# Moving a quarter of a depthwise convolution and its norms beside the attention over a paged cache

## The chip, the cores and the metric

The kernel runs on one core of one Trainium2 chip. The metric is the device time of one execution in microseconds (us), as the median of several runs. In the profile the engines are PE (TensorE, with PEld for its weight loads), DVE (VectorE), ACT (ScalarE), POOL (GpSimd) and SP (SyncE, which issues DMAs). Each engine works through its own list of instructions in order, and engines wait for one another at semaphores.

## The reference

One decoder layer serves a prompt of 1024 rows and 8 sample rows with the same weights. The part that the change touches is the mixer: attention heads (MLA) beside a convolution group, joined by the projection `w_o`.

```python
qn, qr, c_kv, k_r, u = mixer_inputs(xp, ...)          # u: gated 512 channels
attn = mla_prompt(qn, qr, c_kv, k_r, w_uk, w_uv)      # 8 heads over 1024 rows, causal
conv = silu(layer_norm(depthwise_causal_conv(u_ext, conv_w) + conv_b, g, b))   # 31 taps, 512 channels
mix = concatenate([attn, conv]) @ w_o
mk, mv = mem_kv(mem_prompt, w_xk, w_xv)               # 256 memory rows, wanted later by a cross attention
# the 8 sample rows: the same mixer, but the attention reads a paged cache of 4096 past rows a sample,
#   s = q_lat . past_c + q_rope . past_r ;  p = softmax(s) ;  o_lat = p . past_c ;  o = o_lat . w_uv
# then: layer norm, cross attention, layer norm, feed-forward 1024 -> 4096 -> 1024, layer norm
```

All inputs and results are float32. A product of the prompt is made from two rounded parts of each factor (high and low) in three matmuls (`mm3`, lines 150 to 152).

## The kernel before

The program has stages that follow each other; times are from the profiled execution.

1. Projections, 0 to 212 us. PE forms `u`, the latent `cn`, and the queries `qn` (tile `pq`). DVE works through the convolution beside it: `mix<-u,convw,mix`, line 417, one instruction a tap over 128 channels and 1024 rows, 31 taps for each of `NCT` = 4 quarters of the channels (the first tap of a quarter is a `tensor_scalar`, 30 are `scalar_tensor_tensor`), and rotates the queries (lines 356 to 359).
2. Prompt attention, 243 to 439 us (the block `c3`): 8 heads by 8 row tiles, with two-part copies of the latent (`LH`, `LL` from the transposes `trl`), of keys and of probabilities. Five of the nine norms of the convolution (`conv_norm`) are put in at the steps `CLN`. A norm is four transposes of `mix` into a PSUM bank (`tl`, line 427), a copy by ACT (`cln`), row statistics and scaling by DVE with two small POOL instructions (`clr`), four transposes back (`tl`, line 435) and a copy by ACT.
3. Attention over the paged cache, 439 to 723 us (the block `c2`). 16 steps n, two for each sample b (halves e = 0, 1 of its 4096 cache rows). A step transposes cache rows (`trc`, 32 transposes of 128x128, copied by ACT and DVE in turn to `ct`; `trr` for the rotary part), makes half of a product of the memory keys or values (`mk`, 24 matmuls; its weights `kraw` come by DMA, POOL makes `kwh`, DVE `kwl`), and the scores (`main`). After every second step comes the softmax of a sample, a generator in pieces that the loop puts between other work: ACT copies `main` to `mr`, PE gathers it (`st`), DVE takes the maximum (`mx`, `m`, `md`, `ma`) in turns with PE, then `E_`, its sum `sm`, and `sa`. `values(b)` is the product of `E_` with the cache rows (`pv`, 64 matmuls) and a short gathering product (`pv<-summ,ob`). Step 0 also holds `absorb` (query products `tqs`, `tcs`, `tuk`, `tql`, `tsn`) and `memory_in` (transposes `trm`). Two of the other four norms stand in steps 11 to 14, two in a 17th pass of the loop behind the last scores, where the last softmax and values(7) stand too.
4. `silu` over the normed convolution: the first 640 columns just behind the prompt attention, the others behind the load of `w_o`.
5. The projection `w_o` (tile `po`) from 723 us on. It needs `XHb` and `XLb`, the two parts of `mix` (`split_mix`), and the two parts `w_oh`, `w_ol` of its weights. Memory cross attention and feed-forward follow, unchanged.

In the paged loop PE's order is written out by hand (`manual_schedule`); the order of the other engines comes from a scheduler that goes by priorities in program order, and `issue_after(x)` holds an instruction behind x. A PSUM bank belongs to a tag in each stage: `Banks(tr=3, main=1, st=1, pv=1, mk=1, tl=1)` in the loop, so a second tile of a tag with one bank waits until the first one has been copied out. A generator's `next` is one piece of its work; `run(soft)` advances a pending softmax by one piece, `run(ends)` finishes a `values`.

Of the kernel before, what the change touches and what calls it, by code (L numbers as in the profile page):

```python
# [53 lines left out]
CLN = (2, 8, 14, 20, 26)  # L54
# [51 lines left out]
def decoder_step(ctx: ExitStack, tc: tile.TileContext, I: dict, O: dict):  # L106
# [96 lines left out]
    with ExitStack() as c1:  # L203
# [137 lines left out]
        nc.sync.dma_start(O["new_conv_s"][0, :, 0:CK - 2, :], I["state_conv"][0, :, 1:CK - 1, :])  # L341

# [70 lines left out]
        for ct, u in enumerate(us_):  # L413
            acc = mixC[:, ct, 0:S]
            V.tensor_scalar(acc, u[:, 0:S], convw[:, ct, 0:1], cvec[:, 0, ct:ct + 1], op0=ALU.mult, op1=ALU.add)
            for j in range(1, CK):
                V.scalar_tensor_tensor(acc, u[:, j:j + S], convw[:, ct, j:j + 1], acc, op0=ALU.mult, op1=ALU.add)  # L417
            v = mixC[:, ct, S:NT]
            V.scalar_tensor_tensor(v, us[:, ct, :], convw[:, ct, CONV_S:CK], v, op0=ALU.mult, op1=ALU.add)
            V.tensor_scalar(v, v, cvec[:, 0, ct:ct + 1], None, op0=ALU.add)  # L420
# [37 lines left out]
    with ExitStack() as c3:  # L458
# [145 lines left out]
        for n in range(len(seq) + LAG):  # L604
# [28 lines left out]
        with tc.issue_after(mla_end[-1].ins):  # L633
            silu(0, len(CLN) * P)


    with ExitStack() as c2:
# [33 lines left out]
        def absorb():  # L671

            t = ps.tile([P, H, DB], F32, tag="tr", name="tqs")
# [3 lines left out]
            t = ps.tile([P, 3, DB], F32, tag="tr", name="tcs")  # L677
# [5 lines left out]
            for k in range(2):  # L683
                for g in range(2):
                    t = ps.tile([P, 4, P], F32, tag="tr", name="tuk")
# [37 lines left out]
        def columns(b, e):  # L723

            ct = de.tile([P, 2, 4, 512], F32, tag="ct", name="ct")
            for c in range(4):
# [32 lines left out]
        def softmax(b):  # L759
# [27 lines left out]
            sm = dp.tile([P, H], F32, tag="sm", bufs=2, name="sm")  # L787
# [78 lines left out]
        norms = [conv_norm(i, dp, ps, "tl", 2) for i in range(len(CLN), NTL + 1)]  # L866
# [5 lines left out]

        with tc.manual_schedule(engines={mybir.EngineType.PE}):
            for n in range(2 * DB + 1):
                b, e = divmod(n, 2)
                cols = columns(b, e) if b < DB else iter(())
                run(soft)
                next(cols, None)
                if b == DB:
                    norm()  # L880
                run(soft)
                next(cols, None)
                if b == DB:
                    norm()
# [797 lines left out]
```

## Time and profile before

| | |
|---|---|
| median of 3 runs | 1824.02 us (1823.56 to 1827.28) |
| profiled execution | 1826.9 us, of which 1825.1 us span |
| PE busy | 1686.1 us (92%), 12820 instructions |
| DVE busy | 1256.7 us (69%) |
| ACT busy | 614.7 us (34%) |
| POOL busy | 404.4 us (22%) |
| mean granted TensorE clock | 0.961 |

PE is busy 92% of the span. A busy share is a mean over all stages; in a table of the stages (busy time of each engine in a stretch of the span, and the granted clock) one sees in which of them PE waits, and the waits of PE in such a stretch name the engine that came last. A row of the timeline gives the start, the duration, the engine, the line, the operation, the tile written and those read, the count of alike instructions, and in brackets the idle time before and what ended it.

### The profile page before, as it was taken

Reading aid. Unit: us, or ns where it says so; the run is one execution under the profiler, and the core shown is the slowest. Engines: PE = TensorE matmul, PEld = TensorE weight load, DVE = VectorE, ACT = ScalarE, POOL = GpSimd, SP = SyncE. Lnnn points to the kernel's source line nnn. Section 1 sums busy time; section 2 is a strip of 40 time slices with the busy share of each in tenths; the row PEclk is TensorE's granted clock in tenths of the full one; section 3 lists DMA queues with packets and bytes.
Section 4 is the critical chain, followed back from the end, with each engine's and each line's share of the span. In section 5 each row is a group of like instructions: output and inputs, shape, how many; then the busy total and the mean of one; then the engine's idle time right before and its main releaser. Section 6 shows DMA issues by size and latency. Waiting matters only on the chain.

```text
span 1825.1 us, 32021 instructions
## 1 busy us (share of the span) xinstructions
PE 1686.1 (92%) x12820; PEld 1530.9 (84%) x12820; DVE 1256.7 (69%) x2166; ACT 614.7 (34%) x1283; POOL 404.4 (22%) x456
## 2 busy tenths in 40 slices
PE   8999669997899986999999999999999899999995
PEld 8999657886677764888988788999999899998995
DVE  4899988885444445766558576987777666667666
ACT  4112147775222222211134212333333344434322
POOL 0045033223021312311026311222332210002012
PEclk9999879998799997999999999999999999999998
DMA  6211000006155632323324721345444677877744
GB/s 199 58 48 41 1 24 1 1 5 239 58 205 200 253 135 98 128 105 129 121 82 139 248 105 48 117 135 160 148 137 151 202 263 263 289 264 254 249 143 151
DMA packets 154432, 255.38 MB, mean 140 GB/s; under 512 B 12998, under 2 KB 88174, under 8 KB 150179
## 3 DMA queue, kind: packets, MB, share of 16 engines
q1 hardware_dynamic: 146939, 210.56, 34.5%
q0 software_dynamic: 7344, 42.78, 6.2%
q8 instruction: 101, 1.65, 0.4%
q14 instruction: 48, 0.39, 0.1%
HBM read 207.66 MB, written 46.11 MB: 139 GB/s over the span
## 4 chain that ended last, share of the span: by engine, by line
PE 78%; DVE 10%; DMA 6%; ACT 3%; issue 2%; POOL 1%; SPq 0%; DVEq 0%; POOLq 0%; ACTq 0%
PE pd L151 4%; PE pd L152 4%; PE pd L150 4%; PE po L150 3%; PE po L151 3%; PE po L152 3%; PE ua L150 3%; PE ua L152 3%; PE ua L151 3%; PE trc L733 2%; PE px L151 2%; PE px L150 2%; DMA kraw<-in_w_xk 2%; PE px L152 2%; DMA ar<-in_w_down 2%
## 5 line engine op out<-in xcount | busy, mean ns | idle before, releaser
L151 PE MATMUL pd<-bl,ah 128*128 128x252 f32 (+1 forms) x768 | 219.7, 286 | 11.5 <-DVE bl L143 11.3
L150 PE MATMUL pd<-bh,ah 128*128 128x252 f32 (+1 forms) x768 | 219.3, 286 | 5.2 <-ACT bh L137 4.3
L152 PE MATMUL pd<-bh,al 128*128 128x252 f32 (+1 forms) x768 | 218.4, 284 | 1.8 <-DVE al L143 1.8
L151 PEld LDWEIGHTS pd<-bl,ah 128*128 128x128 f32 x768 | 147.3, 192 | 14.0 <-DVE bl L143 13.7
L150 PEld LDWEIGHTS pd<-bh,ah 128*128 128x128 f32 x768 | 147.2, 192 | 5.6 <-ACT bh L137 4.6
L152 PEld LDWEIGHTS pd<-bh,al 128*128 128x128 f32 x768 | 147.3, 192 | 2.0 <-DVE al L143 2.0
L417 DVE SCALAR_TENSOR_TENSOR mix<-u,convw,mix 128x1024 f32<-128x1024 f32 x120 | 148.9, 1273 | 0.1
L143 DVE TENSOR_TENSOR al<-ar,ah 128x1024 fp32r<-128x1024 f32 x48 | 63.7, 1328 | 72.1 <-ACT ah L137 69.9
L137 ACT CAST ah<-ar 128x1024 fp32r<-128x1024 f32 x48 | 50.3, 1048 | 160.8 <-PE pd L151 125.9
L1309 POOL TENSOR_TENSOR us<-uraw 128x512 f32<-128x512 f32 x28 | 43.7, 1579 | 233.2 <-DMA uraw<-in_w_up 163.7
L143 DVE TENSOR_TENSOR uhl<-uraw,uhl 128x512 fp32r<-128x512 f32 x50 | 50.4, 1011 | 45.6 <-ACT uhl L137 45.5
L143 DVE TENSOR_TENSOR bl<-br,bh 128x1032 fp32r<-128x1032 f32 (+2 forms) x64 | 74.1, 1159 | 6.8 <-ACT bh L137 6.8
L733 PE MATMUL trc<-ident,craw 128*128 128x128 f32 x512 | 67.7, 288 | 10.1 <-ACT ct L137 7.0
L733 PEld LDWEIGHTS trc<-ident,craw 128*128 128x128 f32 x512 | 58.2, 147 | 19.2 <-ACT ct L137 7.2
L565 POOL TENSOR_SCALAR pr<-pr,sm 128x384 f32<-128x384 f32 (+4 forms) x64 | 47.9, 750 | 112.5 <-DVE sm L564 67.0
L137 ACT CAST bh<-br 128x1032 fp32r<-128x1032 f32 (+2 forms) x64 | 60.6, 946 | 36.2 <-PE pd L152 27.5
L137 ACT CAST XHb<-tr 128x512 fp32r<-128x512 f32 x32 | 17.7, 588 | 155.4 <-PE tr L957 155.4
L1460 DVE TENSOR_TENSOR hs<-h,h 128x516 f32<-128x516 f32 x80 | 65.6, 851 | 4.6 <-DMA hc<-hs 4.5
L152 PE MATMUL ub<-XHb,uhl 128*128 128x252 f32 (+1 forms) x240 | 67.6, 282 | 0.0
L150 PE MATMUL ub<-XHb,uhl 128*128 128x252 f32 (+1 forms) x240 | 67.6, 282 | 0.0
L151 PE MATMUL ub<-XLb,uhl 128*128 128x252 f32 (+1 forms) x240 | 67.5, 281 | 0.0
L143 DVE TENSOR_TENSOR kwl<-kraw,kwh 128x512 fp32r<-128x512 f32 x32 | 22.1, 691 | 65.3 <-POOL kwh L140 65.3
(550 smaller groups left out, 5744.3 us busy)
## 6 DMA issues: line engine op xcount, KB each, us to landing
ar<-in_w_down SPq DMA_DIRECT2D x96, 512.0 KB, 5.4
br<-hc SPq DMA_DIRECT2D x48, 516.0 KB, 4.6
hc<-hs SPq DMA_DIRECT2D x75, 258.0 KB, 2.1
uraw<-in_w_up SPq DMA_DIRECT2D x32, 512.0 KB, 6.0
X<-x SPq DMA_DIRECT2D x16, 512.0 KB, 2.6
kt<-in_cache_mem_k SPq DMA_DIRECT2D x32, 256.0 KB, 2.9
vsr<-in_cache_mem_v SPq DMA_DIRECT2D x32, 256.0 KB, 2.8
hc<-h SPq DMA_DIRECT2D x30, 258.0 KB, 2.4
```

What stands on the lines that cost most here:

```text
L137: return A.copy(dst, src)
L143: return (V if eng == "v" else G).tensor_tensor(dst, src, ff(hi), op=ALU.subtract)
L150: T.matmul(out, lh, rh, start=start, stop=False, skip_group_check=onto)
L151: T.matmul(out, lh, rl, start=False, stop=False, skip_group_check=onto)
L152: T.matmul(out, ll, rh, start=False, stop=stop, skip_group_check=onto)
L417: V.scalar_tensor_tensor(acc, u[:, j:j + S], convw[:, ct, j:j + 1], acc, op0=ALU.mult, op1=ALU.add)
L565: G.tensor_scalar(pr[:, :w], pr[:, :w], sm[:, 0:1], 1.0, op0=ALU.mult, op1=ALU.mult)
L733: T.transpose(t[:, j, :], raws[b][g // 2][:, (g % 2) * 4 + j, k * P:(k + 1) * P], ident)
L1309: G.tensor_tensor(t, x, y, op=op)
L1460: V.tensor_tensor(t, hh[p, x], hh[p, y], op=op)
```

## The change

- The convolution's fourth quarter (ct = 3, 31 taps) leaves the stretch before the prompt attention. It becomes a generator of 62 half-width instructions (128x512), three of which are asked for by each `convolve()`, four times a step, in the steps 0 to 5 of the paged loop (`CONV_STEPS` = 6), held behind the last DVE copy of the step's `trc`. Its input `u` lies in a pool of its own until the loop's end. The sample rows of that quarter (`conv_s`) stay where they were.
- All nine norms go into the paged loop, from step 6 on: the first half of one in front of the scores, the second half in the next step. None is left in the prompt attention or behind the last scores.
- `silu` of the first 640 columns goes from the end of the prompt attention to step 11, behind the last ACT copy of that step.
- In a step the pieces of the softmax stand elsewhere: `st` behind the first 16 transposes instead of ahead of them, the transposed maximum behind the second 16, the broadcast behind `mk`. In steps 0 to 5 every fourth `trc` takes a bank of `tl`, which no norm uses yet.
- `absorb` and `memory_in` write their PSUM tiles to four banks in turn (`mk`, `main`, `pv`, `tl`) instead of one tag each. Step 0 has no half product of the memory, step 1 has two.
- Behind the last scores there is no 17th pass. values(6) is taken out of step 14 and put there in two halves, one on each side of the matmuls of softmax(7); values(7) gets the bank `main`.
- The load of `w_o` is held by the last scores instead of by softmax(7), `split_mix` by the exponential alone.

```diff
-CLN = (2, 8, 14, 20, 26)
+CONV_STEPS = 6
+EARLY = 5
...
+            if ct < NCT - 1:
+                u = up.tile([P, CK - 1 + NT], F32, tag="u", bufs=NCT - 1, name="u")
+            else:
+                u3p = tc.tile_pool(name="u3", bufs=1, side="left", reuse_waits="tile")
+                u = u3p.__enter__().tile([P, CK - 1 + NT], F32, name="u3")
...
+        def conv(ct, u, width):
+            for j in range(CK):
+                for c in range(0, S, width):
+                    acc, x = mixC[:, ct, c:c + width], u[:, j + c:j + c + width]
...
+                        V.scalar_tensor_tensor(acc, x, convw[:, ct, j:j + 1], acc, op0=ALU.mult, op1=ALU.add)
...
+                    yield
...
-        for ct, u in enumerate(us_):
...
+        for ct in range(NCT - 1):
+            for _ in conv(ct, us_[ct], S):
+                pass
+        conv_s(NCT - 1)
...
-            if n in CLN:
-                with tc.high_priority(offset=0):
-                    for _ in conv_norm(CLN.index(n), ap_, ps, "sc", 1):
-                        pass
...
-        with tc.issue_after(mla_end[-1].ins):
-            silu(0, len(CLN) * P)
...
-                    t = ps.tile([P, 4, P], F32, tag="tr", name="trc")
+                    t = ps.tile([P, 4, P], F32, tag="tl" if more and (2 * c + k) % 4 == 3 else "tr", name="trc")
...
-            pv = ps.tile([P, 512], F32, tag="pv", name="pv")
+            pv = ps.tile([P, 512], F32, tag="main" if b == DB - 1 else "pv", name="pv")
             for tt in range(NTOK):
+                if b == DB - 2 and tt == NTOK // 2:
+                    yield
...
-                    t = ps.tile([P, 4, P], F32, tag="mk", name="trm")
+                    t = ps.tile([P, 4, P], F32, tag=("mk", "main", "pv", "tl")[2 * m + g], name="trm")
...
+        norms = [conv_norm(i, dp, ps, "tl", 2) for i in range(NTL + 1)]
+        rest = conv(NCT - 1, us_[NCT - 1], S // 2)
+        nconv = -(-2 * CK // (4 * CONV_STEPS))
...
+        def convolve():
+            with tc.issue_after(tail["v"].ins):
+                for _ in range(nconv):
+                    next(rest, None)
...
+            for n in range(2 * DB):
                 b, e = divmod(n, 2)
+                cols = columns(b, e, n < CONV_STEPS)
+                next(cols, None)
                 run(soft)
                 next(cols, None)
                 run(soft)
                 run(ends)
+                convolve()
                 if n == 0:
                     absorb()
                     memory_in()
-                next(mem, None)
-                if b == DB or n in (11, 13):
+                else:
+                    next(mem, None)
+                if n == 1:
+                    next(mem, None)
+                if n > CONV_STEPS:
                     norm()
                 run(soft)
+                convolve()
+                if n >= CONV_STEPS:
                     norm()
+                scores(b, e)
+                if n == CONV_STEPS + EARLY:
+                    with tc.issue_after(tail["a"].ins):
+                        silu(0, EARLY * P)
+                convolve()
+                if e == 0 and 0 < b < DB - 1:
                     v = values(b - 1)
                     next(v)
                     ends.append(v)
+                run(soft)
+                convolve()
...
+            ends = [values(DB - 2)]
             run(ends)
+            for _ in range(3):
+                run(soft)
+            run(ends)
+            ends.append(values(DB - 1))
+            next(ends[-1])
+            run(soft)
+            run(ends)
...
-        with tc.issue_after(tail["pa"].ins), tc.issue_after(tail["pv"].ins):
+        with tc.issue_after(tail["pa"].ins):
             for i in range(3):
                 split_mix(i)
+        with tc.issue_after(tail["sc"].ins):
             wts, last = load_square(wp, "w_o")
```

At three places the instructions themselves show the move. The first is DVE's list where the prompt attention begins (`rtq` and `qs` are the rotation of the sample rows' queries, `LL` is the first thing that the attention wants from DVE). Before:

```order
L358 TENSOR_TENSOR qs<-qs,mix 8x8x32
L417 SCALAR_TENSOR_TENSOR mix<-u,convw,mix 128x1024
L359 TENSOR_TENSOR qs<-qs,rtq 8x8x32
L417 SCALAR_TENSOR_TENSOR mix<-u,convw,mix 128x1024 x3
L143 TENSOR_TENSOR LL<-trl,LH 128x512 x2
L475 CAST maskb<-mf 128x128
```

And of the changed kernel, from the sum of the last query tile on:

```order
L430 TENSOR_TENSOR qs<-pq,qs 8x256
L379 TENSOR_TENSOR rtq<-qs,mix 8x8x16
L380 TENSOR_TENSOR rtq<-qs,mix 8x8x16
L381 TENSOR_TENSOR qs<-qs,mix 8x8x32
L382 TENSOR_TENSOR qs<-qs,rtq 8x8x32
L144 TENSOR_TENSOR LL<-trl,LH 128x512 x2
```

No tap of the convolution stands between the last query tile and `LL` any more.

The second place is DVE's list in step 2 of the paged loop, with the softmax of sample 0 (`mx`, `m`, `md`, `ma`, `E_`, `sm`). Before:

```order
L769 TENSOR_REDUCE mx<-st 128x8
L770 TENSOR_TENSOR mx<-mx,SN 128x8
L139 COPY ct<-trc 128x512 x2
L775 TENSOR_REDUCE m_5371<-st 8x1
L777 TENSOR_SCALAR md<-ident,m_5371 8x8
L139 COPY ct<-trc 128x512 x2
L782 COPY ma<-st 128x8
L784 TENSOR_TENSOR E__5409<-st,ma 128x256
L785 TENSOR_TENSOR E__5409<-SN,ma 128x8
L788 TENSOR_REDUCE sm<-E__5409 128x8
L143 TENSOR_TENSOR kwl<-kraw,kwh 128x512
```

And of the changed kernel, from the first copies behind that maximum on:

```order
L140 COPY ct<-trc 128x512 x2
L354 SCALAR_TENSOR_TENSOR mix<-u_865,convw,mix 128x512 x2
L788 TENSOR_REDUCE m_5285<-st 8x1
L354 SCALAR_TENSOR_TENSOR mix<-u_865,convw,mix 128x512 x2
L790 TENSOR_SCALAR md<-ident,m_5285 8x8
L144 TENSOR_TENSOR kwl<-kraw,kwh 128x512
L354 SCALAR_TENSOR_TENSOR mix<-u_865,convw,mix 128x512 x2
L795 COPY ma<-st 128x8
L354 SCALAR_TENSOR_TENSOR mix<-u_865,convw,mix 128x512
L144 TENSOR_TENSOR kwl<-kraw,kwh 128x512
L354 SCALAR_TENSOR_TENSOR mix<-u_865,convw,mix 128x512
L797 TENSOR_TENSOR E__5338<-st,ma 128x256
```

Taps of the convolution and both `kwl` now stand among the steps of the softmax; before, `kwl` stood behind `sm`.

The third place is PE's list behind the last scores (`main`). Before:

```order
L756 MATMUL main<-krt,qrs_4974 32x128 x16
L767 MATMUL st<-summ,mr 128x8x8 x4
L427 MATMUL tl<-ident,mix 128x128 x4
L773 MATMUL st<-ident,mx 8x128
L435 MATMUL tl_7658<-ident,cln 128x128 x4
L780 MATMUL st<-md,ones 128x8
L427 MATMUL tl<-ident,mix 8x128 x4
L791 MATMUL st<-sm,ones 128x8
L435 MATMUL tl_7692<-ident,cln 128x8 x4
L803 MATMUL pv<-craw,E__7667 8x256 x32
L813 MATMUL pv<-summ,ob_4976 128x8 x2
L150 MATMUL po<-w_oh_7778,XHb 128x512 x6
```

And of the changed kernel:

```order
L769 MATMUL main<-krt,qrs_4832 32x128 x16
L817 MATMUL pv<-craw,E__7487 8x256 x16
L780 MATMUL st<-summ,mr 128x8x8 x4
L786 MATMUL st<-ident,mx 8x128
L793 MATMUL st<-md,ones 128x8
L817 MATMUL pv<-craw,E__7487 8x256 x16
L817 MATMUL pv<-craw,E__7696 8x256 x32
L805 MATMUL st<-sm,ones 128x8
L827 MATMUL pv<-summ,ob_4834 128x8 x2
L827 MATMUL pv<-summ,ob_4835 128x8 x2
L151 MATMUL po<-w_oh_7813,XHb 128x512 x6
```

The two norms (`tl`) are gone from here, and the values of sample 6 (`E__7487`) stand around the softmax of sample 7. The count of `pv` is that of the instructions written, 32; the profile shows 64 for them.

## Rows read from the trace of the kernel before

**Rows 1.** Stretches: length, PE, PEld, DVE, ACT, POOL busy, clock, DMA share, GB/s
```profile
180.00:212.00 32.00, 32.00 (x274) 31.72 (x272) 30.16 (x37) 4.46 (x12) 0.00 (x0) 1.00 0.00 1
212.00:243.10 31.10, 0.99 (x4) 0.38 (x3) 30.52 (x44) 1.44 (x3) 0.00 (x0) 0.55 0.06 17
243.10:439.20 196.10, 182.19 (x1233) 154.41 (x1233) 158.63 (x408) 137.53 (x366) 66.60 (x90) 0.97 0.09 33
439.20:480.50 41.30, 25.54 (x133) 22.03 (x134) 14.43 (x37) 11.50 (x19) 6.73 (x13) 0.59 0.39 147
480.50:693.90 213.40, 197.24 (x2208) 153.06 (x2211) 99.44 (x238) 58.93 (x107) 48.63 (x63) 0.97 0.49 178
693.90:723.40 29.50, 15.16 (x147) 8.06 (x147) 12.12 (x21) 8.30 (x16) 8.31 (x9) 0.65 0.24 81
```

**Rows 2.** Timeline of DVE where the prompt attention begins
```profile
212.51 0.41 DVE L407 TENSOR_TENSOR qs<-pq,qs 8x256 f32<-8x256 f32 x1 [2.31 <-ACT qs L405]
...
239.22 3.91 DVE L417 SCALAR_TENSOR_TENSOR mix<-u,convw,mix 128x1024 f32<-128x1024 f32 x3
243.05 1.28 DVE L143 TENSOR_TENSOR LL<-trl,LH 128x512 fp32r<-128x512 f32 x2
```

**Rows 3.** Timeline of PE there
```profile
243.19 0.47 PE L427 MATMUL tl<-ident,mix 128*128 128x128 f32 x1 [8.36 <-DVE mix L417]
```

**Rows 4.** The costliest groups of the page: the convolution's taps
```profile
L417 DVE SCALAR_TENSOR_TENSOR mix<-u,convw,mix 128x1024 f32<-128x1024 f32 x120 | 148.9, 1273 | 0.1
```

**Rows 5.** Groups by line and shape, 243 to 440 us: transposes of the norms
```profile
L435 PE MATMUL tl<-ident,cln 128*128 128x128 f32 x20 | 3.9, 296 | 1.2 <-DVE nm L556 0.6 <-DVE ptl L143 0.5
L427 PE MATMUL tl<-ident,mix 128*128 128x128 f32 x17 | 2.9, 287 | 8.4 <-DVE mix L417 8.4
```

**Rows 6.** Timeline of ACT behind the prompt attention: silu
```profile
441.10 4.46 ACT L443 ACTIVATE mix<-mix,cvec 128x516 f32<-128x516 f32 x8
```

**Rows 7.** Timeline of PE in step 0 of the paged loop
```profile
446.21 4.45 PE L733 MATMUL trc<-ident,craw 128*128 128x128 f32 x20 [7.04 <-ACT ct L137]
...
464.89 1.11 PE L830 MATMUL trm<-ident,min 128*128 128x128 f32 x4
475.08 0.55 PE L150 MATMUL mk<-kwh,MH__4984 128*128 128x256 f32 x1 [1.49 <-DVE ML__4985 L143]
...
480.47 2.25 PE L752 MATMUL main<-ct,qst 128*32 128x512 f32 x16
```

**Rows 8.** Groups by line and shape, 480.4 to 694 us: kwl on DVE
```profile
L143 DVE TENSOR_TENSOR kwl<-kraw,kwh 128x512 fp32r<-128x512 f32 x29 | 20.1, 692 | 58.8 <-POOL kwh L140 58.8
```

**Rows 9.** Waits from 480 to 694 us: total, times, longest
```profile
PE trr L737 <- DVE ct L139: 5.7, 4, 2.2
...
PE st L767 <- ACT mr L761: 4.9, 7, 0.7
```

**Rows 10.** Timeline of POOL beside the convolution's taps
```profile
116.64 0.25 POOL L359 TENSOR_TENSOR cn<-cn,rt 128x32 f32<-128x32 f32 x1
...
147.91 4.98 POOL L359 TENSOR_TENSOR cn<-cn,rt 128x32 f32<-128x32 f32 x1
```

**Rows 11.** Timeline of PE in the loop's last steps and behind them
```profile
682.43 3.64 PE L803 MATMUL pv<-craw,E__7383 128*8 128x256 f32 x64
...
690.79 0.36 PE L150 MATMUL mk<-kwh,MH__4984 128*128 128x256 f32 x1
...
693.83 1.92 PE L752 MATMUL main<-ct,qst 128*32 128x512 f32 x16
...
697.34 1.10 PE L767 MATMUL st<-summ,mr 128*128 128x64 f32 x8 [0.70 <-ACT mr L761]
...
714.14 0.59 PE L435 MATMUL tl<-ident,cln 8*128 8x8 f32 x4 [7.84 <-DVE cln L431]
714.66 6.30 PE L803 MATMUL pv<-craw,E__7667 128*8 128x256 f32 x64
...
723.23 2.24 PE L150 MATMUL po<-w_oh,XHb 128*128 128x512 f32 x5
```

More of the change, by code (lines that the diff above doesn't have):

```diff
@@ L341, in decoder_step, with conv_s @@
         nc.sync.dma_start(O["new_conv_s"][0, :, 0:CK - 2, :], I["state_conv"][0, :, 1:CK - 1, :])
+        def conv(ct, u, width):
+            for j in range(CK):
+                for c in range(0, S, width):
+                    acc, x = mixC[:, ct, c:c + width], u[:, j + c:j + c + width]
+                    if j:
+                        V.scalar_tensor_tensor(acc, x, convw[:, ct, j:j + 1], acc, op0=ALU.mult, op1=ALU.add)
+                    else:
+                        V.tensor_scalar(acc, x, convw[:, ct, 0:1], cvec[:, 0, ct:ct + 1], op0=ALU.mult, op1=ALU.add)
+                    yield
+            if width == S:
+                conv_s(ct)
+        def conv_s(ct):
+            v = mixC[:, ct, S:NT]
+            V.scalar_tensor_tensor(v, us[:, ct, :], convw[:, ct, CONV_S:CK], v, op0=ALU.mult, op1=ALU.add)
+            V.tensor_scalar(v, v, cvec[:, 0, ct:ct + 1], None, op0=ALU.add)
         qcp = tc.tile_pool(name="qc", bufs=1, side="left", reuse_waits="tile")
@@ L671, in absorb @@
         def absorb():
-            t = ps.tile([P, H, DB], F32, tag="tr", name="tqs")
+            t = ps.tile([P, H, DB], F32, tag="pv", name="tqs")
             for h in range(H):
@@ L676, in absorb @@
             V.tensor_scalar(qT, t[:QD], MLA_SCALE, None, op0=ALU.mult)
-            t = ps.tile([P, 3, DB], F32, tag="tr", name="tcs")
+            t = ps.tile([P, 3, DB], F32, tag="tl", name="tcs")
             for k in range(2):
@@ L684, in absorb @@
                 for g in range(2):
-                    t = ps.tile([P, 4, P], F32, tag="tr", name="tuk")
+                    t = ps.tile([P, 4, P], F32, tag=("mk", "main", "pv", "tl")[2 * k + g], name="tuk")
                     for h in range(4):
@@ L721, in window, with columns @@
             return slice(8 - 8 * e, ZW - 8 * e)
-        def columns(b, e):
+        def columns(b, e, more):
             ct = de.tile([P, 2, 4, 512], F32, tag="ct", name="ct")
@@ L786, in softmax @@
             tail["pa"] = A.activation(E_, E_, AF.Exp)
-            sm = dp.tile([P, H], F32, tag="sm", bufs=2, name="sm")
+            sm, sa = (dp.tile([P, H], F32, tag=x, bufs=2, name=x) for x in ("sm", "sa"))
+            probs[b] = E_, sa
             V.reduce_sum(sm, E_[:, :NTOK].rearrange("p t h -> p h t"), axis=AX.X)
@@ L864, in memory_all @@
                 yield
-        norms = [conv_norm(i, dp, ps, "tl", 2) for i in range(len(CLN), NTL + 1)]
+        norms = [conv_norm(i, dp, ps, "tl", 2) for i in range(NTL + 1)]
+        rest = conv(NCT - 1, us_[NCT - 1], S // 2)
+        nconv = -(-2 * CK // (4 * CONV_STEPS))
         mem, soft, ends = memory_all(), [], []
@@ L889, in decoder_step @@
                     memory_in()
-                next(mem, None)
-                if b == DB or n in (11, 13):
+                else:
+                    next(mem, None)
+                if n == 1:
+                    next(mem, None)
+                if n > CONV_STEPS:
                     norm()
                 run(soft)
-                if n in (12, 14) or b == DB:
+                convolve()
+                if n >= CONV_STEPS:
                     norm()
-                if b < DB:
-                    scores(b, e)
-                if e == 0 and b:
+                scores(b, e)
[4 more added lines that the diff above has]
+                if e == 0 and 0 < b < DB - 1:
                     v = values(b - 1)
@@ L904, in decoder_step @@
                     run(soft)
+            ends = [values(DB - 2)]
             run(ends)
-            while norms:
-                norm()
+            for _ in range(3):
[5 more added lines that the diff above has]
+            run(ends)
+        assert not norms and not soft and not ends and next(rest, None) is None
         pmp.__exit__(None, None, None)
         rawp.__exit__(None, None, None)
+        u3p.__exit__(None, None, None)
     spill = ctx.enter_context(tc.tile_pool(name="spill", bufs=1, space=DRAM))
@@ L1041, in split_mix @@
                 split(XH[:, 4 * j:4 * j + 4, cols], XL[:, 4 * j:4 * j + 4, cols], m[:, :, cols], "a", "pv"[j])
-        with tc.issue_after(tail["pa"].ins), tc.issue_after(tail["pv"].ins):
+        with tc.issue_after(tail["pa"].ins):
             for i in range(3):
                 split_mix(i)
+        with tc.issue_after(tail["sc"].ins):
             wts, last = load_square(wp, "w_o")
         with issued_after(last):
-            silu(len(CLN) * P, NT)
+            silu(EARLY * P, NT)
             for i in range(3, NTL):
```

20 lines of the change are left out of this document (1 added, 19 removed).

## The prediction

> **What bounds the kernel now.** The table by stretch comes first, because it shows in which stages PE stands still. Up to 212 us PE is busy without a gap at full clock [rows 1], so nothing taken from DVE there shortens anything. From 212.0 to 243.1 PE works 0.99 us of 31.1 and DVE 30.52: this stretch is DVE's. From 243.1 to 439.2 PE is busy 182.19 of 196.1 us, from 480.5 to 693.9 it is busy 197.24 of 213.4: PE's stages, with 16.2 us of waits in the second. The stretches 439.2 to 480.5 (25.54 of 41.3 us, mean clock 0.59) and 693.9 to 723.4 (15.16 of 29.5, clock 0.65) are bound by turns between engines. Second, the timeline of DVE and PE at 212 to 244 tells what that idle stretch waits for: PE's wait ends at 243.19 behind `mix`, the taps [rows 3], and DVE goes to `LL`, the attention's first need, only at 243.05, behind the last three taps [rows 2]. Third, the timelines of PE and ACT at the other two gaps; fourth, the waits inside the loop. DVE is busy 99.44 of the loop's 213.4 us, 47%, which is the room that the moved taps are to fill.
>
> **The change, part by part.** The sum is made against the profiled execution, 1826.9 us; the median of the runs, 1824.02, is 2.9 below it.
>
> 1. *Start of the attention.* A quarter is 31 taps. Three in a row span 3.91 us, so about 1.27 with the last one's tail or, from 239.22 to 243.05, 1.28 each at most; the mean is 1.273 [rows 2, 4]. Overlapped they start some 1.2 apart, so 31 make 37 us. DVE's list would then end at about 206, which is before PE's last query tile is there: the sum `qs` at 212.51 waited 2.31 us for ACT even now [rows 2]. So PE's side sets the end: `qs`, then the four rotations of the sample rows that the order shows, about 1.4 us by the 0.41 of the one in the row, gives 213.9 for `LL` in place of 243.05: **-29.1**. Some 8 us of the 37 thus buy nothing. If `LL` were held by something later still, up to half could be lost; I keep that as a rival.
>
> 2. *The attention without five norms.* 20 and 17 transposes (three records are missing) keep PE busy 3.9 and 2.9 us [rows 5], 1.36 a norm. PE bounds this stage at 93%, so nearly all of 6.8 counts: **-6.5**. Between -3 (if DVE's turns fill the gap) and -9 (with DVE's and ACT's part).
>
> 3. *Step 0 of the paged loop.* `silu` held ACT from 441.10 to 445.56 [rows 6] and PE's first transposes waited 7.04 us for ACT's copy [rows 7]. Without it they go on at once, about 6 us earlier. The four `trm`, from 464.89 to the start of `mk` at 475.08, took one bank in turn, 10.2 us for four times 1.11 us of work [rows 7]; with four banks only the DMA of the third and fourth input tile is left between them, and I take 7. The 24 matmuls of `mk`, 475.08 to 480.47 at half clock, 5.4 us, are not in step 0 any more. That is 6 + 3 + 5.4 = 14.4. The stretch now holds 12 half taps, some 8 us of DVE, in front of what PE wants; DVE is busy only 14.43 of 41.3 us there [rows 1], so they hide in the main, and I give 2 back: **-12.5**, between -8 and -15.
>
> 4. *The loop.* The second `mk` of step 1 comes back at full clock, 690.79 to 693.83: +3.0. values(6) leaves: -3.6 by its neighbour's 3.64 [rows 11]. Seven more norms (five from the attention, two from the end) at 1.36 us, less for that of 8 rows: +8.5. The wait of `st` for `mr`, 4.9 us in 7 times [rows 9], goes, since transposes stand between: -4.9. `silu` in step 11 holds ACT 4.5 us and a table load on each side; it stands between the last ACT copy and the copy `mr`, where PE has half an `mk` and the scores, 3 + 3 us, to do: +1.5, between 0 and 6. Then the taps. No half-width tap is in the trace; half of 1.2 is 0.60, and the nearest row of that size, `kwl`, is 0.69 [rows 8], so 62 cost DVE 37 to 43 us, 50 of them in steps 1 to 5. A step has 213.4/15 = 14.2 us and 99.44/15 = 6.6 us of DVE work [rows 1]; ten taps bring that to 12.6 to 13.5. It fits, but DVE's list is in order, and of a step 58.8/15 = 3.9 us go to waits of `kwl` for `kwh` [rows 8]. If all of that wait stayed, a step would be 16.5 to 17.4 us, 2.3 to 3.2 too long, 16 us over five steps; if the taps fill the waits, nothing. `kwl` now stands in front of `E_`, about a third of a step later than it stood against its load, which argues for shorter waits. I take half: +8, between 0 and 20. Behind a late DVE the next to wait is PE's `trc`, whose banks DVE empties. The 5.7 us of `trr` [rows 9] I leave as they are. Together **+12.5**, between +2 and +31.
>
> 5. *Behind the last scores.* From `main` at 693.83 to `po` at 723.23 are 29.4 us [rows 11], of them 7.84 for a norm's scaling and 6.30 for values(7) at half clock. In the new order PE has the scores (3.0), values(6) (3.6), `st` (1.1), values(7) (3.6 warm, 6.3 cold) and the short gatherings (1), that is 12.3 to 15, and waits for about three turns with DVE that nothing covers, 0.8 each, and for the copies of `pv`, 1.8: 16.5 to 19.2. I take 17.4: **-12**, between -9 and -14. `split_mix` starts behind the exponential and has some 8 us until `po`.
>
> Sum: -29.1 - 6.5 - 12.5 + 12.5 - 12 = -47.6, so 1779.3 for a profiled execution and 1776.4 for the median; I say **1776**. All good ends give -65 (1759), all bad ones -18 (1806).
>
> **A rule against it.** POOL's `TENSOR_TENSOR` of 128x32 takes 0.25 us, but beside the taps the same instruction took 4.98 [rows 10], as long as four taps. The Trainium skill ("SBUF — State Buffer", section "Who interferes with whom") says that a DVE instruction with two SBUF inputs contends with a GpSimd instruction that reads SBUF, and that the one which starts second is blocked for the whole instruction. Row and rule agree. Every moved tap has two SBUF inputs (`u`, `mix`), and `kwh` on POOL reads SBUF. What that makes here is the first rival.
>
> **Rivals.**
> - *DVE becomes the bound in steps 1 to 5, with POOL shut out by its taps.* Each of ten `kwh` may wait out a train of two half taps, 1.3 us, and `kwl` then waits for it on DVE. Cost 16 (all waits stay) + 13 = 29 in place of 8: 1776 + 21 = **1797**. For it: the 4.98, and an order that puts taps two by two ahead of `kwl`. Against it: as soon as DVE itself stands at `kwl`, POOL is free, and `kwh` takes less than a tap.
> - *The taps cost nothing.* The 3.9 us of waits a step take them in, and `trr` loses its wait as well: 1776 - 8 - 3 = **1765**. For it: 47% busy. Against it: the taps come at fixed places of an ordered list.
> - *The attention can't start at 214.* If something else than the taps holds half of the 31 us (the change then doesn't do what it says): 1776 + 14.5 = **1790**. Against it: DVE is busy 30.52 of the 31.1, and PE's wait names `mix`.
> - *Slower: PE falls to half clock in the loop.* In 439 to 480 us, where PE waits turn by turn, the clock was 0.59; in the loop it is 0.97 [rows 1]. A step at 0.59 costs 14.2 x (0.97/0.59 - 1) = 9.1 us more. From 47.6/9.1 = 5.2 such steps on the kernel is slower; the six steps with taps would give 1776 + 54.6 = **1831**. For it: a PE that waits for DVE in each step. Against it: the loop's four waits of `trr` left the mean at 0.97.
>
> **How the numbers follow.** Forecast 0.55, DVE bound 0.22, taps free 0.10, start held 0.05, half clock 0.08. A measurement of this kernel tells about 0.2%, 3.6 us, from no change. Of the last rival, 0.03 lies in mild forms within that, 0.05 beyond; the others are all faster: 0.92 faster, 0.03 same, 0.05 slower. Range 1758 to 1806: the ends of the sum; it holds forecast and first three rivals, the half clock falls out.
>
> **What would show it.** The attention's first `trl` and `LL` at about 214 (step 1). The stretch of the attention some 6 us shorter (2). `main` of step 0 about 29 us behind the attention's end in place of 41 (3). Steps 1 to 5 of 14 to 17 us with PE near full clock; waits of PE for `ct` from DVE of some 8 us in all; if they are over 20, or `kwl` and `kwh` each wait for the other, the first rival (4). `po` some 17 us behind the last `main` (5). The prediction is wrong if the loop gives back more than 30 us, or if PE is still idle near 214.

## The result, and the profile after

| | before | changed |
|---|---|---|
| median | 1823.79 us (4 runs, 1820.21 to 1827.28) | 1776.93 us (4 runs, 1772.65 to 1782.63) |
| ratio to before | | 0.9745 (0.9712 to 0.9779) |
| span of the profiled execution | 1825.1 us | 1780.8 us |

The forecast was 1776 us for the median. The execution that was profiled is the slowest of the four (1782.63 us), so its stretches add up to some 6 us more than the median. Its span is shorter than before by 44.3 us, and six points of the program tell where: the first `LL` on DVE, the end of the last matmul `o` of the prompt attention, the first, sixth and last block of scores (`main`), and the first `po`.

| stretch | before | changed | difference | forecast |
|---|---|---|---|---|
| to the first `LL` | 243.05 | 213.44 | -29.6 | -29.1 |
| prompt attention | 196.1 | 188.6 | -7.5 | -6.5 |
| step 0, to the first scores | 41.3 | 30.2 | -11.1 | -12.5 |
| first to last scores | 213.4 | 227.1 | +13.7 | +12.5 |
| last scores to `po` | 29.4 | 19.0 | -10.4 | -12 |
| rest | 1101.9 | 1102.5 | +0.6 | 0 |

The table by stretch of the changed kernel, with the columns of [rows 1]; the fifth line is the loop's first five steps, the sixth its last ten:

```profile
180.00:210.90 30.90, 30.90 (x266) 30.81 (x265) 25.52 (x46) 4.09 (x11) 1.49 (x1) 1.00 0.11 35
210.90:213.44 2.54, 1.23 (x12) 0.99 (x9) 1.98 (x7) 1.44 (x3) 0.00 (x0) 1.00 0.00 0
213.44:402.10 188.66, 175.10 (x1198) 148.88 (x1199) 152.91 (x393) 133.01 (x357) 62.20 (x80) 0.98 0.10 37
402.10:432.29 30.19, 19.20 (x105) 16.47 (x103) 21.44 (x47) 4.59 (x8) 5.15 (x11) 0.63 0.46 170
432.29:511.16 78.87, 67.76 (x728) 52.62 (x727) 65.34 (x125) 18.15 (x33) 20.62 (x21) 0.95 0.40 142
511.16:659.37 148.21, 137.10 (x1490) 108.64 (x1489) 77.39 (x182) 53.07 (x96) 38.63 (x57) 0.97 0.50 182
659.37:676.90 17.53, 12.45 (x195) 6.91 (x193) 9.21 (x19) 6.46 (x15) 7.07 (x5) 0.98 0.36 136
```

The 31 us in which PE stood still are 2.5 now. DVE is busy 25.52 of the 30.9 us ahead of that: this is the room that the prediction had found there. What was moved shows in the fifth line: DVE is busy 65.34 of 78.87 us, and PE, with 67.76, waits 11 us. DVE's timeline at the start, answering [rows 2]:

```profile
211.69 0.41 DVE L430 TENSOR_TENSOR qs<-pq,qs 8x256 f32<-8x256 f32 x1 [0.46 <-ACT qs L428]
...
213.09 0.41 DVE L382 TENSOR_TENSOR qs<-qs,rtq 8x256 f32<-8x256 f32 x1
213.44 1.27 DVE L144 TENSOR_TENSOR LL<-trl,LH 128x512 fp32r<-128x512 f32 x2
```

Step 0 on PE, answering [rows 7]:

```profile
401.92 2.56 PE L746 MATMUL trc<-ident,craw 128*128 128x128 f32 x20
...
410.31 1.92 PE L700 MATMUL tuk<-ident,ukn 128*64 128x128 f32 x8 [3.43 <-DVE qT L689]
412.15 3.58 PE L705 MATMUL tql<-qT,ukT 64*128 64x8 f32 x16
420.73 3.58 PE L705 MATMUL tql<-qT,ukT 64*128 64x8 f32 x16 [4.99 <-DVE ql L706]
...
430.31 2.06 PE L844 MATMUL trm<-ident,min 128*128 128x128 f32 x8 [2.00 <-DMA min<-in_mem_prompt]
432.29 2.61 PE L765 MATMUL main<-ct,qst 128*32 128x512 f32 x16
```

The wait of 7.04 us for ACT is gone. Two new ones, for `qT` and `ql`, together 8.4 us, have come, and DVE's list shows what stands in front of both:

```profile
405.55 2.58 DVE L356 TENSOR_SCALAR mix<-u,convw,cvec 128x512 f32<-128x512 f32 x2
408.06 2.06 DVE L354 SCALAR_TENSOR_TENSOR mix<-u,convw,mix 128x512 f32<-128x512 f32 x3
410.05 0.21 DVE L689 TENSOR_SCALAR qT<-tqs 96x64 f32<-96x64 f32 x1
...
417.35 1.09 DVE L144 TENSOR_TENSOR kwl<-kraw,kwh 128x512 fp32r<-128x512 f32 x1 [2.24 <-POOL kwh L141]
418.37 0.74 DVE L354 SCALAR_TENSOR_TENSOR mix<-u,convw,mix 128x512 f32<-128x512 f32 x1
...
420.40 0.27 DVE L706 COPY ql<-tql 128x64 f32<-128x64 f32 x1
```

Five taps stand ahead of `qT`; `kwl`, itself late for a load, and a tap ahead of `ql`. Behind the last scores, answering [rows 11]:

```profile
665.65 0.27 PE L786 MATMUL st<-ident,mx 128*8 128x128 f32 x1 [0.72 <-DVE mx L783]
666.55 0.38 PE L793 MATMUL st<-md,ones 8*128 8x8 f32 x2 [0.63 <-DVE md L790]
...
668.59 3.64 PE L817 MATMUL pv<-craw,E__7696 128*8 128x256 f32 x64
672.16 0.39 PE L805 MATMUL st<-sm,ones 128*128 128x8 f32 x2
675.54 0.61 PE L827 MATMUL pv<-summ,ob 128*128 128x8 f32 x4 [2.99 <-DVE ob L140]
677.48 1.02 PE L827 MATMUL pv<-summ,ob 128*128 128x8 f32 x4 [1.33 <-DVE ob L140]
678.35 2.91 PE L151 MATMUL po<-w_oh,XHb 128*128 128x512 f32 x6
```

values(7) runs at full clock now (3.64 us for 6.30). Two turns with DVE are still waited for, 0.72 and 0.63 us; the third, for `sm`, is hidden behind values(7). The two large waits left, 2.99 and 1.33 us, are DVE's too: three `XLb` stand ahead of its copies `ob`.

```profile
670.31 4.71 DVE L144 TENSOR_TENSOR XLb<-mix,XHb 128x512 fp32r<-128x512 f32 x3 [0.66 <-ACT XHb L138]
```

### The profile page after: what moved, and what is told of

Read it like the earlier page. It is cut to its first block, busy times and chain, and to the rows that moved or that the text cites. A ratio compares the mean times of both kernels' runs of the same rounds, so it can differ in the third digit from the quotient of the medians.

```text
span 1780.8 us, 32063 instructions
## 1 busy us (share of the span) xinstructions
PE 1680.2 (94%) x12820; PEld 1529.6 (86%) x12820; DVE 1267.7 (71%) x2197; ACT 614.8 (35%) x1283; POOL 402.1 (23%) x456
## 4 chain that ended last, share of the span: by engine, by line
PE 76%; DVE 9%; DMA 7%; issue 3%; ACT 3%; POOL 1%; SPq 0%; DVEq 0%; POOLq 0%; ACTq 0%
PE pd L152 4%; PE pd L153 4%; PE pd L151 4%; PE po L151 3%; PE po L152 3%; PE po L153 3%; PE ua L151 3%; PE ua L153 3%; PE ua L152 3%; DMA ar<-in_w_down 2%; PE trc L746 2%; PE px L152 2%; PE px L151 2%; PE px L153 2%; PE ub L152 2%
## 5 line engine op out<-in xcount | busy, mean ns | idle before, releaser
L152 PE MATMUL pd<-bl,ah 128*128 128x252 f32 (+1 forms) x768 | 220.1, 287 | 10.3 <-DVE bl L144 10.1
L354 DVE SCALAR_TENSOR_TENSOR mix<-u,convw,mix 128x1024 f32<-128x1024 f32 (+1 forms) x150 | 154.6, 1067 | 0.2
L584 POOL TENSOR_SCALAR pr<-pr,sm 128x128 f32<-128x128 f32 (+3 forms) x64 | 47.6, 748 | 116.4 <-DVE sm L583 69.4
L138 ACT CAST XHb<-tr 128x512 fp32r<-128x512 f32 x32 | 17.8, 589 | 154.5 <-PE tr L992 154.4
L1431 POOL TENSOR_TENSOR ar<-ar,ar 128x1024 f32<-128x1024 f32 x8 | 20.2, 2523 | 197.1 <-DMA ar<-in_w_down 181.3
```

Source lines behind the costliest of these rows:

```text
L138: return A.copy(dst, src)
L152: T.matmul(out, lh, rl, start=False, stop=False, skip_group_check=onto)
L354: V.scalar_tensor_tensor(acc, x, convw[:, ct, j:j + 1], acc, op0=ALU.mult, op1=ALU.add)
L584: G.tensor_scalar(pr[:, :w], pr[:, :w], sm[:, 0:1], 1.0, op0=ALU.mult, op1=ALU.mult)
L1431: G.tensor_tensor(x, x, y, op=ALU.subtract)
```

## The experiments

The experiments were timed in five rounds against the kernel before, in three sessions (the first four, the next four, the last three), each with its own runs of the kernel before; between sessions the ratios compare better than the medians. Stretches come from one profiled execution each, and two kernels show how far such a stretch can be trusted: "late start" and "late start, late `ob`" are the same program up to the last scores, and still differ by 2.0 us in steps 1 to 5 and by 5.2 in the last ten. In the six kernels that hardly differ there (changed, late start, late `ob`, full width, full late, early taps) the last ten steps took 141.6 to 148.2 us. So less than some 6 us in that column, and some 2 us in that of steps 1 to 5, is not read as an effect.

| kernel | median us | ratio (interval) | to `LL` | attention | step 0 | steps 1-5 | last ten | to `po` |
|---|---|---|---|---|---|---|---|---|
| changed | 1776.93 | 0.9745 (0.9712-0.9779) | 213.4 | 188.6 | 30.2 | 78.9 | 148.2 | 19.0 |
| no taps | 1764.73 | 0.9683 (0.9659-0.9707) | 213.9 | 187.9 | 25.6 | 70.0 | 143.1 | 18.8 |
| taps back | 1795.04 | 0.9843 (0.9819-0.9868) | 240.8 | 190.5 | 25.9 | 70.3 | 145.8 | 18.8 |
| kwh on ACT | 1776.14 | 0.9737 (0.9710-0.9763) | 213.8 | 187.8 | 27.7 | 76.5 | 145.5 | 18.7 |
| late start | 1771.97 | 0.9710 (0.9681-0.9738) | 213.8 | 188.2 | 20.7 | 80.5 | 148.2 | 20.8 |
| taps and norms back | 1790.18 | 0.9840 (0.9825-0.9855) | 243.0 | 194.8 | 26.2 | 69.9 | 135.3 | 19.0 |
| full width | 1771.26 | 0.9730 (0.9713-0.9747) | 213.7 | 187.9 | 26.4 | 78.5 | 141.6 | 18.8 |
| old order | 1793.05 | 0.9841 (0.9827-0.9855) | 213.7 | 187.9 | 29.0 | 86.3 | 152.2 | 18.8 |
| late start, late `ob` | 1767.74 | 0.9711 (0.9695-0.9728) | 213.7 | 188.4 | 21.1 | 78.5 | 143.0 | 17.8 |
| and full width | 1766.61 | 0.9679 (0.9648-0.9709) | 213.8 | 188.7 | 20.5 | 77.6 | 145.0 | 17.8 |
| and early taps | 1763.29 | 0.9665 (0.9636-0.9694) | 214.8 | 188.5 | 21.2 | 75.0 | 144.5 | 17.8 |
| and `kwh` on ACT | 1762.06 | 0.9658 (0.9628-0.9688) | 214.9 | 187.9 | 21.4 | 71.3 | 142.9 | 17.8 |

**What the moved taps cost: left out.**

```diff
-            for j in range(CK):
+            for j in range(CK if width == S else 1):
```

> This kernel leaves out 60 of the 62 moved taps (the fourth quarter of the convolution gets its first tap only); all else is the changed kernel (1776.9 us; attention's end to the first scores 30.2 us, first to sixth scores 78.9 us, sixth to last scores 148.2 us). Theory A (taps stand in DVE's ordered list in front of what PE waits for): step 0 falls to about 25 us, the five steps to about 70, the last ten stay within 1 us; in all 13 to 15 us less, about 1763. Theory B (taps fill DVE's waits and cost nothing): no stretch moves by more than 2 us, about 1775.

12 us less. Step 0 gave 4.6 us (the two taps that are left stand ahead of `qT`, where PE still waits 1.43 us), steps 1 to 5 gave 8.9; theory A holds, taps are not free. The table by stretch of this kernel (steps 1 to 5, the last ten):

```profile
427.33:497.31 69.98, 66.68 (x728) 51.82 (x727) 32.37 (x75) 18.15 (x33) 16.71 (x21) 0.94 0.46 159
497.31:640.36 143.05, 134.07 (x1490) 105.71 (x1489) 77.37 (x182) 53.07 (x96) 38.58 (x57) 0.99 0.51 188
```

DVE is busy 32.37 us in place of 65.34. Of these 33 us of taps PE paid 8.9: three quarters were hidden. Where PE paid shows in its waits in steps 1 to 5 of the changed kernel (total us, times, longest):

```profile
PE st L786 <- DVE mx L783: 3.1, 1, 3.1
PE pv L817 <- ACT E__5338 L799: 2.4, 1, 2.4
PE trc L746 <- DVE ct L140: 1.9, 3, 0.8
PE mk L152 <- DVE kwl L144: 1.6, 2, 1.3
PE mk L151 <- POOL kwh L141: 1.1, 1, 1.1
```

Without the taps only `kwh`, 2.5 us, and two waits of 0.5 and 0.3 us are left. So the taps are waited for mostly in the turns of the softmax (`mx`, and `E_`, which ACT gets late from DVE), and little at the banks of `trc`.

**The taps back ahead of the attention.**

```diff
-        for ct in range(NCT - 1):
+        for ct in range(NCT):
...
-        conv_s(NCT - 1)
...
-        rest = conv(NCT - 1, us_[NCT - 1], S // 2)
+        rest = iter(())
```

> The fourth quarter is convolved in full width ahead of the prompt attention again, as before; norms, silu, PE's new order and the new tail stay. The forecast's view of the start (DVE's list alone sets it): LL at 243 in place of 213.4, +29.6. Theory A (the moved taps cost the loop some 14 us): the loop gets these back, so the whole is about 1777 + 29.6 - 14 = 1792. Theory B (they cost nothing there): 1806. If the start is held by something else: under 1785.

`LL` came at 240.80, 27.4 us later, and step 0 with steps 1 to 5 gave back 13: by theory A. Not all of the taps stand ahead of `LL` here, though: two have gone behind it (at 242.00 and 244.14). And PE's row of step 0 shows that the wait for `ql` is there without any tap in that step, behind `kwl`:

```profile
240.80 1.27 DVE L144 TENSOR_TENSOR LL<-trl,LH 128x512 fp32r<-128x512 f32 x2
242.00 1.26 DVE L354 SCALAR_TENSOR_TENSOR mix<-u,convw,mix 128x1024 f32<-128x1024 f32 x1
```

```profile
445.28 3.58 PE L704 MATMUL tql<-qT,ukT 64*128 64x8 f32 x16 [5.79 <-DVE ql L705]
```

So the taps' move alone is worth 18 us (1795.0 to 1776.9), the rest of the change 29 (1823.8 to 1795.0).

**POOL shut out by the taps?**

```diff
-                split(wh, wl, raw, "p", "v")
+                split(wh, wl, raw, "a", "v")
```

> kwh, the rounded memory weights, is made by ACT in place of POOL, in all steps; the taps stay. Theory A (what PE waits for in steps 1 to 5 is DVE's own ordered list): first to sixth scores stay within 3 us of 78.9, the whole within 4 of 1777. Theory C (POOL is shut out by taps with two SBUF inputs, kwh comes late and holds kwl on DVE): these steps fall by 6 to 13 us, the whole to about 1768.

Steps 1 to 5 fell by 2.3 us, hardly more than their scatter, and the whole not beyond its interval. The lock itself is in the changed kernel's rows; three of POOL's in steps 2 and 3 of the loop:

```profile
453.80 0.62 POOL L141 TENSOR_SCALAR kwh<-kraw 128x512 fp32r<-128x512 f32 x1 [3.90 <-DMA kraw<-in_w_xv]
459.39 2.00 POOL L141 TENSOR_SCALAR kwh<-kraw 128x512 fp32r<-128x512 f32 x1 [4.97 <-DVE mix L354]
463.48 1.17 POOL L141 TENSOR_SCALAR kwh<-kraw 128x512 fp32r<-128x512 f32 x1 [2.10 <-DVE mix L354]
```

A `kwh` of 0.62 us takes 1.17 and 2.00 beside taps. But PE waited for `kwh` or `kwl` 2.7 us in all in steps 1 to 5. The first rival's mechanism is there, and only a small part of its price.

**Step 0: taps behind `absorb`.**

```diff
+            tail["sn"] = V.tensor_copy(SN, t)
...
-                split(wh, wl, raw, "p", "v")
+                cast("p", wh, raw)
+                with tc.issue_after(tail["sn"].ins):
+                    lows("v", wl, raw, wh)
...
-            with tc.issue_after(tail["v"].ins):
+            with tc.issue_after(tail["sn" if n == 0 else "v"].ins):
...
-                convolve()
                 if n == 0:
                     absorb()
                     memory_in()
+                convolve()
```

> In step 0 all taps and the kwl of the memory weights are held behind SN, the last DVE result of absorb; nothing else stands between on DVE. Theory A: PE's waits of 3.4 us (for qT, behind five taps) and 5.0 us (for ql, behind kwl and a tap) go; the stretch from the attention's end to the first scores falls from 30.2 to about 24.5, the whole to about 1771. Theory D (the input tiles of the memory and their DMA decide that stretch anyway): 0 to -2.

Step 0 took 20.7 us, 9.5 less; the 1.6 that steps 1 to 5, which take over taps, are longer is within their scatter. By the ratios the whole gained 0.35%, and the intervals overlap. PE's rows of this kernel for the two places where 3.43 and 4.99 us had stood, and what bounds the step now:

```profile
408.23 1.95 PE L705 MATMUL tql<-qT,ukT 64*128 64x8 f32 x16 [0.62 <-DVE ukT L701]
411.72 2.75 PE L705 MATMUL tql<-qT,ukT 64*128 64x8 f32 x16 [1.55 <-DVE ql L706]
...
420.53 2.15 PE L844 MATMUL trm<-ident,min 128*128 128x128 f32 x8 [2.06 <-DMA min<-in_mem_prompt]
```

**Five norms back in the attention** (on top of the taps back, with which alone the attention can norm early; the edit, of which the lines on norms are shown, also puts the quarter's `u` back into the pool of the others).

```diff
+            if n in CLN:
+                with tc.high_priority(offset=0):
+                    for _ in conv_norm(CLN.index(n), ap_, ps, "sc", 1):
+                        pass
...
-        norms = [conv_norm(i, dp, ps, "tl", 2) for i in range(NTL + 1)]
+        norms = [conv_norm(i, dp, ps, "tl", 2) for i in range(len(CLN), NTL + 1)]
```

> On top of the kernel with the taps back (1795.0 us; attention 190.5, steps 1 to 5 70.3, last ten steps 145.8): five norms stand in the prompt attention again at their old steps, four are left in the loop, so that this pair differs in the place of five norms alone. Theory A (a norm costs PE the same 1.3 us in either place): attention +6.5, loop -6.5, whole within 3 us of 1795. Theory E (the loop hides them in its waits, so their move was a gain): attention +6.5, loop within 2, whole about 1801.

Start and attention grew by 2.2 and 4.3 us, in sum the 6.5 that both theories had. The 2.2 is the place of two taps: all 31 stand ahead of `LL` again, at 243.04, as before the change. The whole stayed (0.9840 for 0.9843), where theory E had some 6 us more: it falls, the loop does not hide the norms. The last ten steps shrank by 10.5:

```profile
527.48:673.27 145.79, 136.50 (x1491) 108.28 (x1490) 77.18 (x182) 53.08 (x96) 38.58 (x57) 0.96 0.50 182
```

```profile
533.82:669.14 135.32, 129.36 (x1451) 101.38 (x1450) 70.48 (x167) 47.93 (x86) 34.65 (x47) 0.99 0.54 198
```

The first fence is the last ten steps with all nine norms in the loop, the second with four. PE works 7.1 us less and waits 3.3 us less. But the granted clock differs, 0.96 and 0.99. The norms' own transposes (`tl`; busy time of PE, PEld and ACT in the same two stretches) give a cleaner price:

```profile
527.48:673.27 145.79, 10.10 (x72) 7.70 (x72) 9.58 (x17) 0.96 0.50 182
```

```profile
533.82:669.14 135.32, 4.39 (x32) 3.30 (x32) 4.07 (x8) 0.99 0.54 198
```

That is 5.7 us of PE for five norms, 1.14 each. The kernel without taps has all nine norms in the loop, too, and took 143.05 us for these steps at 0.99, 7.7 more than with four. That norms cost more in the loop than in the attention is therefore not shown. The one wait that goes is that of `trc` for ACT's `ct`:

```profile
PE trc L745 <- ACT ct L138: 3.4, 1, 3.4
```

It stands behind `silu`, which in the loop with all norms starts only after two of the norms' copies (in the changed kernel they start at 599.65 and 600.12, `silu` at 602.04).

**Full-width taps.**

```diff
-        rest = conv(NCT - 1, us_[NCT - 1], S // 2)
+        rest = conv(NCT - 1, us_[NCT - 1], S)
-        nconv = -(-2 * CK // (4 * CONV_STEPS))
+        nconv = itertools.cycle((2, 1, 1, 2))
```

> The changed kernel with the moved quarter in 31 full-width taps (128x1024) instead of 62 halves, five or six a step in the same steps. Theory A, if DVE's sum of work decides (a full tap costs 1.2, two halves 1.35): 31 x 0.15 = 4.7 us less DVE work, first to sixth scores 78.9 falls to about 75. Theory F, if it is where a tap stands (a result that PE waits for comes up to a whole tap later, 1.2 in place of 0.68): the same stretch is 3 to 8 us longer, and the whole about 1782.

Neither: steps 1 to 5 stayed (78.5), and the whole is not beyond its interval (0.9730 for 0.9745). Step 0 fell by 3.8 us, where fewer taps stand ahead of `qT` and `ql`. DVE saves what was expected (30 taps 38.6 us, for 43.3 of 60 halves), and no harm shows from a result that comes a whole tap late.

**The softmax at its old places.**

```diff
                 cols = columns(b, e, n < CONV_STEPS)
+                run(soft)
                 next(cols, None)
                 run(soft)
                 next(cols, None)
...
-                run(soft)
                 convolve()
                 if e == 1:
```

> The changed kernel with the pieces of the softmax at their old places in a step (st ahead of the first 16 transposes, transposed maximum behind them, broadcast ahead of mk, its sum behind mk). Forecast's view: st waits 0.7 us for ACT's copy mr again in seven steps, +4.9, whole about 1782. Rival: beside the taps the softmax needs the earlier start, so that the new order is what makes DVE's lateness show; then the wait for E_ in steps 2 and 4 (2.4 and 0.3 us) goes and the whole is 1774 to 1778.

Slower by 16 us (1793.05; by the spans of the two profiled executions 11.4), over three times the 4.9 that the wait for `mr` had promised. In steps 1 to 5, 7.4 us longer, it is not the wait alone; a table by stretch and PE's rows of step 2 (`sm` is the sum that stands ahead of the scores again):

```profile
430.57:516.87 86.30, 73.32 (x727) 55.39 (x727) 66.15 (x125) 18.15 (x33) 18.20 (x21) 0.88 0.38 133
```

```profile
464.58 0.60 PE L805 MATMUL st<-sm,ones 128*128 128x8 f32 x2 [2.91 <-DVE sm L802]
465.11 3.64 PE L765 MATMUL main<-ct,qst 128*32 128x512 f32 x16
468.52 1.94 PE L769 MATMUL main<-krt,qrs 128*32 128x128 f32 x32
```

DVE has the same 66 us of work. But PE stands 2.91 us for `sm`, which stands behind taps, and what follows runs at the lower of the clock's two levels: the same scores took 1.92 and 1.06 us elsewhere. The mean granted clock is 0.88 for 0.95, PE busy 73.3 for 67.8 us. So 5.6 of the 7.4 us are PE's own work at a lower clock. In the new order `st<-sm` stands behind the scores and the values and is not waited for in these steps; in step 2 the values wait 2.4 us for `E_` instead.

**The end: `ob` on ACT** (on top of the late start).

```diff
-                cast("av"[c % 2], ob[r], pv[r, 0:LAT])
+                cast("av"[c % 2] if b < DB - 2 else "a", ob[r], pv[r, 0:LAT])
```

> The kernel with a late start of the taps in step 0 (1772.0), and for samples 6 and 7 all four copies ob of the values on ACT instead of two on DVE, where they stand behind XLb (4.7 us beside POOL's XLb). If that place in DVE's list makes the last gathering wait (3.0 and 1.3 us before the two pv<-summ,ob): from the last scores to po 19 to 21 us falls to about 17, whole about 1769. If w_oh or XHb sets po's start: unchanged.

17.8 us from the last scores to `po`, for 20.8 with the late start alone and 19.0 in the changed kernel. By the ratios the whole did not gain (0.9711 for 0.9710). The waits for DVE went; 2.15 us for ACT and 1.44 for `w_oh` came in their place:

```profile
657.69 0.59 PE L827 MATMUL pv<-summ,ob 128*128 128x8 f32 x4
660.43 0.61 PE L827 MATMUL pv<-summ,ob 128*128 128x8 f32 x4 [2.15 <-ACT ob L138]
662.48 2.93 PE L151 MATMUL po<-w_oh,XHb 128*128 128x512 f32 x6 [1.44 <-POOL w_oh L141]
```

**Together.** Full width on top of the last, then six full-width taps ahead of the attention and 25 in the loop, then `kwh` on ACT:

```diff
+        rest = conv(NCT - 1, us_[NCT - 1], S)
+        for _ in range(6):
+            next(rest)
...
-        nconv = itertools.cycle((2, 1, 1, 2))
+        nconv = itertools.chain((2,) * 1, itertools.repeat(1))
```

> The late start of the taps in step 0 and the copies ob on ACT (1767.7), now with 31 full-width taps. Theory A (less DVE work, 4.7 us of some 42, in a stretch where DVE is busy 65 of 79 us): first to sixth scores from 78.5 to about 76, whole about 1765. If the gain of full width (1771 against 1777) was that of step 0 alone (30.2 to 26.4), which the late start has taken already: nothing more, 1767 to 1768.

> The same, with the first six full-width taps of the quarter ahead of the prompt attention, 25 left for the loop. The prediction said that some 8 of the 37 us there buy nothing, since DVE waits for PE's last query tiles. If so: LL stays within 1 us of 213.7, step 0 and steps 1 to 5 together fall by a fifth of what taps cost there (13 us), 2 to 3 us, whole about 1763. If DVE had no such room: LL up to 7 us later, no gain or a loss.

> The same with kwh on ACT in place of POOL. By the run with kwh on ACT alone (1 us less, steps 1 to 5 2.3 us less) another 0 to 2 us, whole about 1762; ACT is busy under 40% there, so nothing against it. If ACT's list (ct, mr, the exponential) is held by kwh's wait for its DMA: 3 to 8 us more.

Full width gave 1 us, within its interval: the late start had taken that gain. The early taps moved `LL` by 1.0 us, to 214.79, and shortened steps 1 to 5 by 2.6, little more than their scatter: the room at the start is real, its worth small. `kwh` on ACT gave another 3.7 us in steps 1 to 5, more than alone. None of these single steps is beyond the interval of the whole; their sum is. The last kernel, 1762.06 us, 0.9658 (0.9628 to 0.9688), is the best here: about 15 us below the changed one. Its steps 1 to 5:

```profile
424.14:495.41 71.27, 65.82 (x727) 51.62 (x726) 55.34 (x95) 23.70 (x43) 10.31 (x11) 0.97 0.47 166
```

With 55.34 us of DVE it takes 1.3 us more than the kernel without taps.

## Why the prediction was right, and where only its sum was

1. *Start.* Right in mechanism and size: `LL` at 213.44 for 213.9 forecast. That some 8 of the 37 us buy nothing was shown from both sides: with all 31 taps ahead of it (norms back) `LL` comes 29.6 us later, not 37, and six full-width taps ahead of it moved it by 1.0. The rival of a start held by something else is out.
2. *Attention.* -7.5 for -6.5. The norms' transposes, 6.8 us of PE by the prediction's rows, are gone from it, and with the norms back start and attention together took 6.5 us more.
3. *Step 0.* -11.1 for -12.5, with two terms off. What the removals gave was larger than 14.4: without taps the stretch is 25.6, 15.7 shorter than before. And the taps did not hide: they took 4.6 where 2 were given, and together with `kwl` 9.5, as the mended order shows. The failed sentence is "DVE is busy only 14.43 of 41.3 us there [rows 1], so they hide in the main": the idle time lay in turns with PE, and of the 4.5 us that five taps stood in front of `qT` PE waited 3.43. The wait for `ql` the prediction did not have at all; it is the work of `kwl`, whose weights come late by DMA, more than of the tap beside it (5.79 us with no tap in step 0).
4. *Loop.* +13.7 for +12.5. Taps: +8 forecast, 8.9 measured in steps 1 to 5, the right size by another path. The prediction named PE's `trc`, held by DVE's copies `ct`, with some 8 us as the wait to look for; it was 1.9 us there, and the softmax's turns and the memory weights took the rest. That this number fitted is in part luck. `silu`: +1.5 forecast, 3.4 measured, since norms' copies on ACT stand ahead of it. Norms: +8.5 forecast for seven; the transposes `tl` keep PE busy 10.1 us in the loop for 2.5 before, so 7.6. The order of the softmax: -4.9 forecast for the waits for `mr`, and these are gone from the changed kernel. Beside the taps the order is worth more than that: with the old one steps 1 to 5 were 7.4 us longer (the last ten by 4, which alone would not be read) and the whole 16. The prediction, which took order and taps as terms of their own, did not have this part: the turn for `sm` ahead of the scores, which the taps lengthen, and the clock behind it.
5. *End.* -10.4 for -12: the new order did what it was to do, and of the three turns two were waited for, 0.72 and 0.63 us, less than the 0.8 each of the sum. The copies of `pv` were not 1.8 us but two waits of 4.3 behind `XLb`. The late `ob` got 1.2 of it back, then `w_oh` was next.

Of the rivals, the taps as the bound of DVE with POOL shut out showed its mechanism (2.00 us for a `kwh` of 0.62), and 2.3 us in place of 13. The Trainium skill, "SBUF — State Buffer", "Who interferes with whom", has a DVE instruction with two SBUF inputs contend with a GpSimd instruction that reads SBUF; those rows bear it out. That taps are free is out by the kernel without them. The half clock did not come in the loop of the changed kernel (0.95 in steps 1 to 5), but in mild form with the old order (0.88).

What stays open: why the last ten steps vary by 6 us among kernels that hardly differ there. A part of it goes with the granted clock: 148.21 us with PE busy 137.10 at 0.97 in the changed kernel, 143.05 with 134.07 at 0.99 in the one without taps. Why the clock differs is not shown.

## What to carry to other kernels

Work moved beside a bound engine is paid for by where its pieces stand in an ordered list, not by the busy share of the stretch: 33 us of taps cost PE 9, and in step 0 five of them cost it 3.4. Give the moved pieces the places in which nobody waits for what is behind them, and give the bound engine other work ahead of each result that they make late; here that reordering was worth nearly as much as the move itself. A sum can come right though a term was paid at another place than the one it was reckoned at, so measure its terms one at a time before the next change rests on them.

## What the runs showed that was not expected

- The first two half taps, `TENSOR_SCALAR` of 128x512 from one input, took 2.58 us together, 1.33 each, more than a two-input tap of that size (0.75), beside the gathers and small memsets that POOL issues. With the late start, where these are over, the same two took 1.08 us; a first tap of full width took 2.41 us at the early place and 0.81 in the projections. The rows point to POOL's work; nothing was changed to test it alone.
- A half tap took 0.75 us, 0.66 to 0.69 apart, at the upper end of the estimate (0.60 to 0.69).
- Three `XLb` on DVE beside three on POOL took 4.71 us, where `kwl`, of the same operation and size, took 0.69 each.
